# Two-row modulation runs, full-height blocks for the retention layer's 32 new tokens, full-row attention scores in the first half, and a new order table, in a one-core streaming-encoder step

## Chip, core and metric

The kernel runs on one core of one Trainium2 chip. Its metric is the device time of one execution in microseconds (us), lower being better. The core has five engines with instruction streams of their own: TensorE (PE in the profile; its weight loads are listed apart, as PEld), VectorE (DVE), ScalarE (ACT), GpSimd (POOL) and SyncE (SP, which here issues transfers). Each stream is static: an engine takes its instructions in the written order and waits at semaphores.

## The reference

One step of a two-layer streaming encoder on 512 prompt tokens and 32 new tokens, with 1024 features and fp32 throughout. Layer 0 mixes tokens by retention (8 heads, keys of 128, values of 256, a decayed state per head); after it one shared K and V is projected; layer 1 is differential attention (8 heads, each with two 64-wide halves) against that K and V. Each layer has a half-step SwiGLU FFN on either side of its mixer, a norm around each part, and shift, scale and gate from a conditioning vector.

```python
def modulate(x, g, shift, scale):
    return rms_norm(x, g) * (1 + scale[:, None, :]) + shift[:, None, :]

def swiglu(h, w_in, w_out):
    a, b = jnp.split(h @ w_in, 2, axis=-1)
    return (jax.nn.silu(a) * b) @ w_out

def retention_block(state, q, k, v, log_gamma):
    ...
    scores = jnp.einsum('bhid,bhjd->bhij', q, k) * d_intra
    out = (jnp.einsum('bhij,bhjv->bhiv', scores, v)
           + jnp.einsum('bhid,bhdv->bhiv', q * q_dec[..., None], state))
    new_state = state * c_dec[:, None, None] + jnp.einsum('bhjd,bhjv->bhdv', k * k_dec[..., None], v)
    return out, new_state
...
        logits = jnp.einsum('bqhtd,bkhtd->bhtqk', qblk, k).astype(jnp.float32) * (DH_B ** -0.5)
        p = jax.nn.softmax(jnp.where(visible, logits, -jnp.inf), axis=-1)
        pd = (p[:, :, 0] - lam * p[:, :, 1]).astype(v.dtype)
        return jnp.einsum('bhqk,bkhv->bqhv', pd, v)
```

The prompt passes through retention in chunks of 64 tokens, and the new tokens through one `retention_block` with the state that is given. The modulation is `silu(c) @ w_ada + b_ada`, nine vectors of 1024 for each layer and two for the shared K and V.

## The kernel before

**Layout.** Features lie on the 128 partitions and tokens on the columns. The tokens are in two halves: half 0 has 256 prompt tokens, half 1 the other 256 prompt tokens and the 32 new ones, 288 columns. Half 1 trails half 0 through the layers, so that one half's projections fill TensorE while the other waits for a norm.

**Main projections.** Weights come in tiles of 512 KB (eight contraction steps k, 128 features each; 384 KB for the last part of an FFN's down projection), issued by SP. ACT casts a tile to a high part (L576), DVE subtracts to get a low part (L579); four such pairs of slots, `WT`, exist. A *unit* is one 128-wide output feature block of one tile; with a half it is one run, `run_unit`: per k three matmuls (high weight by high and low operand, low weight by high operand, L597) into one PSUM bank. Five banks (ps_146 to ps_150 in the names) serve these runs, three (ps_151 to ps_153) everything else. A tile that both halves use closely after one another is cast once for both.

**Who sets the order.** A program at build time makes the order. `plan()` interleaves the units of both halves along a path, whose corner points come from the tables `BND` (layer 0, the shared K and V) and `ATT` (layer 1; `Q` is the query projection, `OB` the output projection of attention, `F2` the second FFN). Then a list scheduler with its own costs per instruction (`pe`, `act`, `dve`, `WAKE` and so on) lays every engine's stream down. `launch()` hands a unit a weight tile and a bank in planned order. The costs only shape the order; nothing of them runs.

**Around a projection.** `pre_ops` makes the operands of the next projection from the residual: the sum of squares over features goes to TensorE as a matmul with ones (L702), its power is taken by POOL (L708), the result is spread over the partitions by a transpose (L713), then per feature block a DVE multiply (L740), an ACT copy to the high part (L749) and a DVE subtraction (L755). Each output bank of a down projection is added up by DVE (L907 and L909) and squared and summed (L815, L819) on the way to the next such norm; `sub_end` applies that norm and adds to the residual (L868, L871). SwiGLU parts end in DVE and ACT steps that split the product again (L920, L921, L940 to L956).

**Modulation, L503.** For each of 9 pieces of 512 outputs per group, eight contraction steps, four matmuls each of 32 columns of the array (`PS[b][32*g:32*g+32]`, four column groups side by side). A step needs 1 MB of weights in one of two buffers (`NADA = 2`); a step was one entry of TensorE's order, so that most steps stood alone between main matmuls.

**Retention.** Per head: rotation of q and k (L1012 to L1026), transposes of v (`post_v`, L1071) and k (`ktok`, L1113), scores (L1202, L1203), outputs (L1219 to L1222), state (L1232), and `finish`, which norms and transposes back (L1172). The new tokens are a block of 32: their scores have 32 columns of the array (L1268), their outputs are a 32-column and a 32 by 32 matmul (L1277, L1278), their state update takes 32 rows (L1284), and their transposes are 32 wide.

**Attention scores.** Per head and block of 128 tokens, two matmuls of 64 rows each (L1535): q's halves stand on partitions 0 to 63 and 64 to 127, the two products go to two of the three misc banks. Mask (L1545), maximum (L1550), exponent (L1555), transposes (L1568), product with v (L1575), sub-norm (L1592, L1596), transpose to features (L1604) and the split for the output projection (L1610) follow. q is rotated with its rows permuted to match the K that is kept, which four transfers of 32 rows bring in (`ldk`).

Behind the change every line stands a few further down; those that matter are L503 (then L504), L597 (L599), L702 (L711), L713 (L722), L740 (L749), L755 (L764), L819 (L828), L868 and L871 (L877, L880), L909 (L918), L921 (L930), L941 (L950), L953 (L962), L579 (L581), L1604 (L1630).

## Time and profile before

| what | value |
|---|---|
| time, median of 3 runs | 2592.47 us (2589.95 to 2595.69) |
| time of the profiled execution | 2587.47 us |
| its span | 2585.5 us |
| mean TensorE clock granted in it | 0.995 |
| PE busy | 2515.2 us, 97% |
| DVE busy | 1415.6 us, 55% |
| ACT busy | 1088.6 us, 42% |
| moved by DMA | 408.41 MB, mean 158 GB/s |

The profiled execution is one run; its times are read against its own 2587.47 us, which is 1.98 us more than its span and 5.0 us less than the median. The engine rows give the time in which an engine was busy. TensorE's weight loads overlap its matmuls. The ends of matmuls are modelled, so that a matmul's own length overlaps the next one by a little; what a matmul costs is read from the starts of successive rows.

### The profile page before, as it was taken

To read this page: it belongs to the slowest core of one execution; us is meant where nothing else is said; L and a number is where in the kernel's file an instruction comes from. 1 tells how busy PE (TensorE), PEld (TensorE's weight loads), DVE (VectorE), ACT (ScalarE), POOL (GpSimd) and SP (SyncE) were. 2 spreads that over 40 slices of the span, in tenths; PEclk is the share of its full clock that TensorE was granted. 3 is DMA by queue.
4 is the path that set the end of the run, shared out by engine and by line. 5 is a ranking of instruction groups with operands and counts; after the bars stand their busy time and mean duration, and the time that the engine had idled before them with its cause. 6 is when DMAs were issued, how large, how long until landed. Compare 5 with 4: busy or idle time off the path is not lost.

```text
span 2585.5 us, 48240 instructions
## 1 busy us (share of the span) xinstructions
PE 2515.2 (97%) x19848; PEld 2366.4 (92%) x19848; DVE 1415.6 (55%) x2659; ACT 1088.6 (42%) x2150; POOL 57.6 (2%) x88
## 2 busy tenths in 40 slices
PE   6999999999999999999999999999999999999998
PEld 5899999789999997899998999999788988888998
DVE  5323336945424366323337945556875987658455
ACT  3222225643333364323126533444445655455434
POOL 0000000000000000000000000000000000000000
PEclk9999999999999999999999999999999999999999
DMA  8722224732222238622225754555754445545553
GB/s 338 265 90 86 87 99 137 263 128 95 78 86 81 74 134 333 245 83 90 99 78 196 256 182 134 171 177 182 277 198 147 152 158 179 176 151 168 166 169 108
DMA packets 123627, 408.41 MB, mean 158 GB/s; under 512 B 15504, under 2 KB 34064, under 8 KB 113168
## 3 DMA queue, kind: packets, MB, share of 16 engines
q1 hardware_dynamic: 123408, 405.35, 46.1%
q8 instruction: 155, 2.54, 0.4%
q14 instruction: 64, 0.52, 0.1%
HBM read 392.05 MB, written 13.24 MB: 157 GB/s over the span
## 4 chain that ended last, share of the span: by engine, by line
PE 64%; DVE 5%; DMA 2%; ACT 1%; issue 1%; POOL 0%; SPq 0%; POOLq 0%; DVEq 0%; ACTq 0%
PE ps L597 57%; DMA FA<-in_ada 1%; DVE w L579 1%; PE ps L503 1%; PE ps L1535 1%; ACT w L576 1%; PE ps L1575 1%; DVE r L755 1%; DVE FA L740 1%; DVE FA L1016 0%; PE ps L1702 0%; PE ps L1568 0%; DVE FA L819 0%; PE ps L1682 0%; PE ps L1642 0%
## 5 line engine op out<-in xcount | busy, mean ns | idle before, releaser
L597 PE MATMUL ps<-r,w 128*128 128x256 f32 (+1 forms) x17280 | 2274.9, 291 | 19.4 <-ACT r L920 4.9
L597 PEld LDWEIGHTS ps<-r,w 128*128 128x128 f32 x17280 | 2203.9, 191 | 92.8 <-issue 59.0
L579 DVE TENSOR_TENSOR w<-FA,w 128x1024 fp32r<-128x1024 f32 (+1 forms) x559 | 667.5, 1195 | 589.5 <-ACT w L576 586.9
L576 ACT CAST w<-FA 128x1024 fp32r<-128x1024 f32 (+1 forms) x559 | 572.2, 1024 | 949.6 <-PE ps L597 852.4
L956 DVE TENSOR_TENSOR FA<-ps,FA 128x256 f32<-128x256 f32 (+1 forms) x88 | 38.8, 441 | 172.4 <-PE ps L597 168.4
L920 ACT CAST r<-FA 128x256 fp32r<-128x256 f32 (+1 forms) x176 | 72.9, 416 | 107.3 <-DVE FA L956 85.9
L909 DVE TENSOR_TENSOR FA<-ps,FA 128x288 f32<-128x288 f32 (+1 forms) x144 | 62.7, 439 | 100.3 <-PE ps L597 98.8
L921 DVE TENSOR_TENSOR r<-FA,r 128x256 fp32r<-128x256 f32 (+1 forms) x176 | 76.5, 437 | 21.3 <-ACT r L920 21.2
L503 PE MATMUL ps<-FA,SC 128*32 128x512 f32 x576 | 77.0, 610 | 5.9 <-DMA FA<-in_ada 5.9
L749 ACT ACTIVATE r<-FA,MOD 128x256 fp32r<-128x256 f32 (+1 forms) x168 | 63.1, 436 | 43.7 <-DVE FA L740 43.5
L819 DVE TENSOR_TENSOR FA<-FA 128x256 f32<-128x256 f32 (+1 forms) x168 | 72.8, 435 | 13.0 <-ACT FA L815 11.5
L953 DVE SCALAR_TENSOR_TENSOR FA<-ps,FA 128x288 f32<-128x288 f32 (+1 forms) x88 | 38.3, 439 | 46.5 <-PE ps L597 46.3
L740 DVE SCALAR_TENSOR_TENSOR FA<-X,DRV,ps 128x256 f32<-128x256 f32 (+1 forms) x168 | 57.5, 396 | 8.8 <-PE ps L713 8.6
L849 ACT ACTIVATE FA<-FA,DRV 128x256 f32<-128x256 f32 (+1 forms) x144 | 59.1, 442 | 2.9
L755 DVE SCALAR_TENSOR_TENSOR r<-FA,MOD,r 128x256 fp32r<-128x256 f32 (+1 forms) x168 | 58.6, 400 | 3.1 <-ACT r L749 3.0
L944 ACT ACTIVATE FA<-ps 128x256 f32<-128x256 f32 (+1 forms) x88 | 34.5, 393 | 60.1 <-PE ps L597 60.0
L708 POOL TENSOR_TENSOR FA<-FA,NHALF 128x2 f32<-128x2 f32 (+1 forms) x24 | 19.9, 831 | 1748.1 <-DVE FA L706 926.2
L1016 DVE TENSOR_TENSOR FA<-ps,FA 64x288 f32<-64x288 f32 (+1 forms) x128 | 56.1, 438 | 2.1
L907 ACT COPY FA<-ps 128x288 f32<-128x288 f32 (+1 forms) x96 | 36.2, 380 | 43.2 <-PE ps L597 43.2
L1012 DVE TENSOR_TENSOR FA<-ps,FA 128x256 f32<-128x256 f32 (+1 forms) x64 | 28.0, 438 | 47.1 <-PE ps L597 46.7
L815 ACT ACTIVATE FA<-FA 128x256 f32<-128x256 f32 (+1 forms) x84 | 35.8, 426 | 14.9 <-DVE FA L909 14.4
L941 DVE SCALAR_TENSOR_TENSOR FA<-FA,ps 128x288 f32<-128x288 f32 (+1 forms) x88 | 37.7, 430 | 6.1 <-ACT FA L940 6.1
(145 smaller groups left out, 1083.0 us busy)
## 6 DMA issues: line engine op xcount, KB each, us to landing
FA<-in_w_ffn_in SPq DMA_DIRECT2D x266, 512.0 KB, 3.3
FA<-in_ada SPq DMA_DIRECT2D x80, 1024.0 KB, 7.1
FA<-in_w_ffn_out SPq DMA_DIRECT2D x96, 512.0 KB, 3.5
FA<-in_w_in_a SPq DMA_DIRECT2D x60, 512.0 KB, 3.2
FA<-in_w_ffn_out SPq DMA_DIRECT2D x61, 384.0 KB, 3.1
FA<-in_w_kv SPq DMA_DIRECT2D x23, 512.0 KB, 3.5
FA<-in_w_out_a SPq DMA_DIRECT2D x22, 512.0 KB, 3.4
FA<-in_w_q_b SPq DMA_DIRECT2D x16, 512.0 KB, 3.6
```

Source lines behind the costliest of these rows:

```text
L503: te.matmul(PS[b][32 * g:32 * g + 32, :], lhsT=SC[:, k, :], rhs=fa(ada_buf[u, k], 512, g * 512), start=(k == 0), stop=(k == 7))
L576: yield act(n, lambda: nc.scalar.copy(hi, src))
L579: yield dve(n, lambda: nc.vector.tensor_tensor(lo, src, hi.bitcast(F32), ALU.subtract))
L597: te.matmul(PS[b][:, :n], lhsT=w[:, a, k, :], rhs=x, start=(k == 0 and j == 0), stop=(k == u.nk - 1 and j == 2))
L740: nc.vector.scalar_tensor_tensor(fa(z, c1 - c0, o), X[:, f, c0:c1], DRV[:, gi, f, s:s + 1], PS[Rb][:, o:o + c1 - c0], ALU.mult, ALU.mult)
L749: nc.scalar.activation(op.hi(H, c0, c1), fa(z, c1 - c0, o), AF.Identity, bias=MOD[:, mi, f, s:s + 1])
L755: nc.vector.scalar_tensor_tensor(op.lo(H, c0, c1), fa(z, c1 - c0, o), MOD[:, mi, f, s:s + 1], op.hi(H, c0, c1).bitcast(F32), ALU.add, ALU. ...
L819: yield dve(n, lambda: nc.vector.tensor_tensor(acc, acc, fa(t), ALU.add))
L849: nc.scalar.activation(Y[:, f, c0:c1], Y[:, f, c0:c1], AF.Copy, scale=DRV[:, gg, f, s:s + 1])
L909: yield dvp(n, lambda: nc.vector.tensor_tensor(Y[:, f, c], PS[b][:, :n], Y[:, f, c], ALU.add), 15)
L920: yield act(n, lambda: nc.scalar.copy(op.hi(H), src), pr)
L921: yield dve(n, lambda: nc.vector.tensor_tensor(op.lo(H), src, op.hi(H).bitcast(F32), ALU.subtract), pr)
```

## The change

Four things change, and the order of everything is made anew.

**Modulation.** `ADA_K = 2`: one entry of TensorE's order now takes two contraction steps, and hands both buffers back behind the second. The same matmuls are done.

```diff
-            for k in range(8):
-                yield ada_ev[u, k]
-
-                def mm(u=u, k=k, b=b):
-                    for g in range(4):
-                        te.matmul(PS[b][32 * g:32 * g + 32, :], lhsT=SC[:, k, :],
-                                  rhs=fa(ada_buf[u, k], 512, g * 512), start=(k == 0), stop=(k == 7))
-                yield pe(980, mm, ADA_HI if u <= due[0] else ADA_LO)
-                ada_put(u, k)
+            for k0 in range(0, 8, ADA_K):
+                for k in range(k0, k0 + ADA_K):
+                    yield ada_ev[u, k]
+
+                def mm(u=u, k0=k0, b=b):
+                    for k in range(k0, k0 + ADA_K):
+                        for g in range(4):
+                            te.matmul(PS[b][32 * g:32 * g + 32, :], lhsT=SC[:, k, :],
+                                      rhs=fa(ada_buf[u, k], 512, g * 512), start=(k == 0), stop=(k == 7))
+                yield pe(TILED + ADA_K * 900, mm, ADA_HI if u <= due[0] else ADA_LO)
+                for k in range(k0, k0 + ADA_K):
+                    ada_put(u, k)
```

**Retention.** The 32 new tokens become the last 32 rows of a full block of 128 (the 96 prompt tokens ahead of them are computed along and not used; in the decay table and the masked scores they have zeros). All transposes and matmuls of that block are then 128 by 128, v and the scaled k are evacuated in one instruction rather than two, and DVE clears a 128 by 128 score block first.

```diff
+    LB = COLS[1].stop - COLS[1].start - P
+    SB = NTOK - P
+    def full_blocks(H):
+        return ((0, P), (P, P), (LB, P))[:2 + H]
...
-            yield pe(c_f(32, 32), lambda: te.matmul(PS[b][:NS_TOK, :NS_TOK], lhsT=V("k")[:, c0:c0 + NS_TOK],
-                                                           rhs=V("q")[:, c0:c0 + NS_TOK], start=True, stop=True), 500)
+            yield dve(P // 2, lambda: nc.vector.memset(sm, 0.0))
+            yield pe(c_f(P), lambda: te.matmul(PS[b][:, :NS_TOK], lhsT=V("k")[:, SB:], rhs=V("q")[:, c0:c0 + NS_TOK],
+                                               start=True, stop=True), 500)
...
-                te.matmul(o, lhsT=fa(qs, NS_TOK), rhs=V("st"), start=True, stop=False)
-                te.matmul(o, lhsT=fa(qs, NS_TOK, NS_TOK, 0, NS_TOK), rhs=vt()[:NS_TOK, 4, :], start=False, stop=True)
+                te.matmul(o, lhsT=qd, rhs=V("st"), start=True, stop=False)
+                te.matmul(o, lhsT=sm, rhs=vt()[:, 4, :], start=False, stop=True)
...
-            yield pe(c_f(256), lambda: te.matmul(PS[b2][:, :256], lhsT=kt()[:NS_TOK, 4, :], rhs=vt()[:NS_TOK, 4, :],
+            yield pe(c_f(256), lambda: te.matmul(PS[b2][:, :256], lhsT=kt()[:, 4, :], rhs=vt()[:, 4, :],
```

**Scores of half 0.** ACT makes two copies of q, each with the other half's rows at zero, and both products are matmuls of all 128 rows, into one bank; mask and maximum are one instruction each. Half 0's q and K need no permutation: 16 pairs of rotation steps on 32 rows fall away, and K comes by one transfer of 128 rows rather than four of 32. Half 1 is as before.

```diff
+            def cp():
+                for s in range(2):
+                    nc.scalar.activation(q3[:, s, :], qT, AF.Copy, scale=CT[:, C_MK + s:C_MK + s + 1])
+            yield ("ACT", 2 * c_act(P) + 180, cp)
+            bs = [(yield from anyb())]
+            l3 = PS[bs[0]][:, :2 * nk].rearrange("p (s n) -> p s n", s=2)
+            lg = [l3[:, 0], l3[:, 1]]
+            def qk():
+                for s in range(2):
+                    te.matmul(lg[s], lhsT=q3[:, s, :], rhs=kT[:, :nk], start=True, stop=True)
+            yield pe(2 * c_f(nk), qk, 500 + h)
```

**Tables and costs.** `TILED = 190` is added to the planner's cost of runs that use part of the array; `WAKE` 100 to 200, `ROPE_LEAD` 18 to 30, `CONV_P` -1 to 0, `ADA_LEAD` -40 to -52, `RETH` 3 to 4; `BND` and `ATT` have new numbers, of which one line:

```diff
-BND = {(0, 1): (7, 7, 7, 13), (0, 2): (6, 7, 8, 7), 'kv': (7, 8, 6, 7), (1, 0): (2, 2, 4, 6)}
+BND = {(0, 1): (7, 7, 6, 10), (0, 2): (7, 7, 6, 5), 'kv': (8, 8, 6, 8), (1, 0): (0, 1, 4, 6)}
```

In sum the modulation now stands in TensorE's order as 36 entries of 8 matmuls, where 66 of 4 and 3 of 8 stood; tiles cast fall from 559 to 552, and the DVE stream from 2661 instructions to 2606; ACT's goes from 2008 to 2017.

What the order looks like now at three places, which the prediction calls Q, end and OB:

*Q* is the start of layer 1's attention, where half 0's norm has to be finished before its query projection starts. TensorE there, before (ps_147 and ps_150 are half 1's down projection, ps_146 half 0's query projection, ps_153 the modulation, ps_152 the norm):

```order
L713 MATMUL ps_151<-CT,FA 128x128 x2
L597 MATMUL ps_147<-r_16_123,w_144 128x288
...
L503 MATMUL ps_153<-FA,SC 32x512 x8
L597 MATMUL ps_150<-r_2_109,w_144 128x288
...
L503 MATMUL ps_153<-FA,SC 32x512 x4
L702 MATMUL ps_152<-ONE,FA 32x2 x8
L713 MATMUL ps_152<-CT,FA 128x128 x2
L503 MATMUL ps_153<-FA,SC 32x512 x4
L597 MATMUL ps_146<-r_20_93,w_141 128x256
```

The same place after the change, nothing left out:

```order
L722 MATMUL ps_152<-CT,FA 128x128 x2
L599 MATMUL ps_150<-r_22_129,w_144 128x288
L599 MATMUL ps_150<-r_23_130,w_144 128x288
L599 MATMUL ps_150<-r_22_129,w_144 128x288
L599 MATMUL ps_150<-r_10_117,w_144 128x288
L599 MATMUL ps_150<-r_11_118,w_144 128x288
L599 MATMUL ps_150<-r_10_117,w_144 128x288
L504 MATMUL ps_151<-FA,SC 32x512 x8
L711 MATMUL ps_153<-ONE,FA 32x2 x8
L722 MATMUL ps_153<-CT,FA 128x128 x2
L599 MATMUL ps_146<-r_20_93,w_141 128x256
```

Between one norm's spreading transpose and the next norm's sums stood 39 main matmuls (15 and 24) and 12 of the modulation; now 6 and 8 stand there.

*End* is the last part of the last FFN, half 0, beside which DVE makes half 1's operands. DVE there, before (L909 with ps_148 and ps_150 empties banks for the next units; L953 and L921 make the last operands of half 0):

```order
L755 SCALAR_TENSOR_TENSOR r_7_114<-FA,MOD,r_6_113 128x256
L755 SCALAR_TENSOR_TENSOR r_7_114<-FA,MOD,r_6_113 128x32
L755 SCALAR_TENSOR_TENSOR r_17_124<-FA,MOD,r_16_123 128x256
L755 SCALAR_TENSOR_TENSOR r_17_124<-FA,MOD,r_16_123 128x32
L953 SCALAR_TENSOR_TENSOR FA<-ps_146,FA 128x256
L921 TENSOR_TENSOR r_11_84<-FA,r_10_83 128x256
L909 TENSOR_TENSOR FA<-ps_148,FA 128x256
L909 TENSOR_TENSOR FA<-ps_150,FA 128x256
```

And after; the 30 rows left out hold 25 further L749 and L764 steps (12 of 256 columns, 13 of 32) and five L581:

```order
L962 SCALAR_TENSOR_TENSOR FA<-ps_147,FA 128x256
L930 TENSOR_TENSOR r_23_96<-FA,r_22_95 128x256
L930 TENSOR_TENSOR r_11_84<-FA,r_10_83 128x256
L715 TENSOR_SCALAR FA<-ps_153 96x3
L918 TENSOR_TENSOR FA<-ps_150,FA 128x256
L581 TENSOR_TENSOR w_143<-FA,w_143 128x768
L749 SCALAR_TENSOR_TENSOR FA<-X,DRV,ps_153 128x256
...
L749 SCALAR_TENSOR_TENSOR FA<-X,DRV,ps_153 128x256
L749 SCALAR_TENSOR_TENSOR FA<-X,DRV,ps_153 128x32
L918 TENSOR_TENSOR FA<-ps_149,FA 128x256
```

The last operands have moved ahead of the block of L749 and L764, and one bank's emptying, that of ps_149, stays inside it.

*OB* is where half 0's attention output goes into its projection. TensorE before: the last head's transpose (L1604), and on the next row the main matmul that uses it:

```order
L597 MATMUL ps_148<-r_14_87,w_141 128x256
L1575 MATMUL ps_151<-FA 128x128 x2
L1604 MATMUL ps_153<-CT,FA 128x128 x2
L597 MATMUL ps_150<-r_30_103,w_142 128x256
L597 MATMUL ps_150<-r_31_104,w_142 128x256
```

After, the same transpose is followed by half 1's units (288 columns), and half 0's first output unit comes 184 rows later:

```order
L599 MATMUL ps_150<-r_14_121,w_143 128x288
L1630 MATMUL ps_153<-CT,FA 128x128 x2
L599 MATMUL ps_150<-r_30_137,w_143 128x288
...
L599 MATMUL ps_146<-r_2_109,w_144 128x288
...
L599 MATMUL ps_147<-r_8_81,w_141 128x256
```

The last head's whole chain now has other matmuls beside it, where its transpose and the matmul that uses it stood back to back.

More of the change, by code (lines that the diff above doesn't have):

```diff
@@ L34 @@
 C_KD = 192
-C_KDS = 208
 C_CO = 216
@@ L46 @@
 L0 = 1
-WAKE = 100
+WAKE = 200
 STREAM = 3
@@ L1141, in finish @@
         def finish(b, H, c0, n):
-            blks = ((0, P), (P, P)) if n == 256 else ((0, n),)
-            rows = blks[0][1]
-            nb = len(blks)
+            rows = P
+            nb = 2 if n == 256 else 1
+            w, o = (n, 0) if n == 256 else (P, P - n)
             og = yield from get(2 * n)
@@ L1171, in tr @@
                     for j in range(2):
-                        te.transpose(PS[b][:, j * n + i * P:j * n + i * P + rows],
-                                     fa(tk, P, 256 * i + j * P, 0, rows), CT[:rows, C_ID:C_ID + rows])
+                        te.transpose(PS[b][:, j * w + i * P:j * w + i * P + P], fa(tk, P, 256 * i + j * P), ID)
             yield pe(2 * nb * c_t(P), tr, 500)
@@ L1431, in post_q @@
                 yield at["qask"][H]
-                yield from rot(H, b, at["rope"], fa(at["q"][H], n, h * n), m=256)
+                yield from rot(H, b, at["rope"], fa(at["q"][H], n, h * n), m=256 * H)
                 S.set(at["hd"][h][H].q)
@@ L1524, in at_block @@
         yield ("get", at["bsem"], 1, 8 * H + h)
-        mem = yield from get(2 * nk + P + 16, h + H * .5)
+        mem = yield from get(2 * nk + P + 16 + (1 - H) * 256, h + H * .5)
         cut = lambda o, n: (mem[0] + o, n)
@@ L1529, in at_block, with qk @@
         p3 = fa(pp).rearrange("p (s n) -> p s n", s=2)
-        bs = yield ("get", miscb, 2, 0)
-        lg = [PS[b][:, :nk] for b in bs]
-        def qk():
-            for s in range(2):
-                te.matmul(lg[s], lhsT=qT[64 * s:64 * s + 64, :], rhs=kT[64 * s:64 * s + 64, :nk], start=True,
-                          stop=True)
-        yield pe(max(440, c_f(nk) + 10), qk, 500 + h)
+        if H:
+            bs = yield ("get", miscb, 2, 0)
+            lg = [PS[b][:, :nk] for b in bs]
+            def qk():
+                for s in range(2):
+                    te.matmul(lg[s], lhsT=qT[64 * s:64 * s + 64, :], rhs=kT[64 * s:64 * s + 64, :nk], start=True,
+                              stop=True)
+            yield pe(TILED + c_f(nk), qk, 500 + h)
+        else:
+            q3 = fa(cut(2 * nk + P + 16, 256)).rearrange("p (s m) -> p s m", m=P)
+            def cp():
[5 more added lines that the diff above has]
+            lg = [l3[:, 0], l3[:, 1]]
+            def qk():
+                for s in range(2):
+                    te.matmul(lg[s], lhsT=q3[:, s, :], rhs=kT[:, :nk], start=True, stop=True)
+            yield pe(2 * c_f(nk), qk, 500 + h)
         at["left"][H] -= 1
@@ L1543, in mask @@
         def mask():
-            for s in range(2):
-                nc.vector.memset(lg[s][0:64, nk - 64:], -3.0e38)
+            if H:
+                for s in range(2):
+                    nc.vector.memset(lg[s][0:64, nk - 64:], -3.0e38)
+            else:
+                nc.vector.memset(l3[0:64, :, nk - 64:], -3.0e38)
         yield ("DVE", 2 * c_dve(64), mask)
         def mx():
-            for s in range(2):
-                nc.vector.tensor_reduce(fa(m, 1, s), lg[s], AX.X, ALU.max, negate=True)
-        yield ("DVE", 2 * c_dve(nk), mx)
+            if H:
+                for s in range(2):
+                    nc.vector.tensor_reduce(fa(m, 1, s), lg[s], AX.X, ALU.max, negate=True)
+            else:
+                nc.vector.tensor_reduce(fa(m, 2), l3, AX.X, ALU.max, negate=True)
+        yield ("DVE", (1 + H) * 67 + 2 * nk / 0.96, mx)
         def ex():
@@ L1709, in at_sample @@
         b = yield from anyb()
-        yield pe(c_f(P), lambda: te.transpose(PS[b][:, :64], fa(t, P, P, 0, 64), CT[:64, C_ID:C_ID + 64]), 500)
+        yield pe(TILED + c_t(P), lambda: te.transpose(PS[b][:, :64], fa(t, P, P, 0, 64), CT[:64, C_ID:C_ID + 64]), 500)
         for j in range(2):
@@ L1799 @@
 DMA_LAT = 2500
-ROPE_LEAD = 18
+TILED = 190
+ADA_K = 2
+ROPE_LEAD = 30
 ADA_X = 4
@@ L1812 @@
 ADA_FIRST = 0
-ADA_LEAD = -40
+ADA_LEAD = -52
 ARENA_N = 20600
 YW = 2
-RETH = 3
+RETH = 4
 ATH = 3
```

77 lines of the change are left out of this document (37 added, 40 removed).

## Prediction

> **What bounds the kernel now.** I read the page's engine rows first, then TensorE's waits, the chain that ended last, and TensorE's timeline where the change acts. The page:
>
> ```profile
> PE 2515.2 (97%) x19848; PEld 2366.4 (92%) x19848; DVE 1415.6 (55%) x2659; ACT 1088.6 (42%) x2150; POOL 57.6 (2%) x88
> GB/s 338 265 90 86 87 99 137 263 128 95 78 86 81 74 134 333 245 83 90 99 78 196 256 182 134 171 177 182 277 198 147 152 158 179 176 151 168 166 169 108
> FA<-in_w_ffn_in SPq DMA_DIRECT2D x266, 512.0 KB, 3.3
> FA<-in_ada SPq DMA_DIRECT2D x80, 1024.0 KB, 7.1
> ```
>
> TensorE is busy for 97% of the span and no other engine for more than 55%, so the time is TensorE's work plus its waits. What it waits for (total us, times, longest):
>
> ```profile
> PE ps L702 <- DVE FA L819: 16.7, 7, 11.5
> PE ps L503 <- DMA FA<-in_ada: 5.9, 11, 1.4
> ```
>
> The waits are few and stand at stage borders. The price of a main matmul comes from a long undisturbed stretch: of 288 columns from the chain's last link (start, us, count), of 256 columns from TensorE's timeline (start, us, instruction, count).
>
> ```profile
> 2367.69 205.15 PE ps L597 x1551
> ```
>
> ```profile
> 2320.69 13.23 PE L597 MATMUL ps<-r,w 128*128 128x256 f32 x108
> 2333.85 0.36 PE L702 MATMUL ps<-ONE,FA 128*32 128x2 f32 x18
> ```
>
> 205.15/1551 is 0.132 us; (2333.85 - 2320.69)/108 is 0.122 us. The main matmuls are the same in number after the change. So three things can move the time: TensorE's other work, what it loses when it turns to that work and back, and the waits at borders. All prices below are distances between starts, since ends are modelled.
>
> **Modulation.** A step alone, then two in a row:
>
> ```profile
> 1018.51 2.25 PE L597 MATMUL ps<-r,w 128*128 128x288 f32 x15
> 1020.69 1.07 PE L503 MATMUL ps<-FA,SC 128*32 128x512 f32 x8
> 1021.68 5.30 PE L597 MATMUL ps<-r,w 128*128 128x288 f32 x39
> ...
> 968.32 1.92 PE L503 MATMUL ps<-FA,SC 128*32 128x512 f32 x16
> 970.17 4.93 PE L597 MATMUL ps<-r,w 128*128 128x256 f32 x39
> ```
>
> The 15 main matmuls ahead of the lone step should take 15 x 0.132 = 1.985 us and its start comes 2.18 us behind theirs: 0.195 us are lost in turning to a run that uses the array in column groups. The step is 0.99 us, so alone it costs 1.185. Two in a row are 1.85, with one turn 2.045. A pair saves 2 x 1.185 - 2.045 = 0.325 us. Of 66 lone steps 33 new pairs are made: 33 x 0.325 = 10.7 us. If the turn is lost anyway the saving is 2 x 0.99 - 1.85 = 0.13, in all 4.3. I take 10.7, since the lost 0.195 shows directly. The Trainium skill's page "TensorEngine Tiling (Array Packing)", Tiling Modes, Key Properties, says that a change of tiling mode drains TensorE; the 0.195 agrees, and by that rule 10.7 is the right end.
>
> The pair needs both its loads, and both buffers come free only behind it. Two loads are 2.1 MB; at the highest slice of the page, 338 GB/s, 6.2 us, and 512 KB with its 1.55 us at that rate lands after 3.3, so 1.75 are fixed: 8.0 us. In the new order most pairs stand 8.8 to 10.3 us of other TensorE work apart (counts by the prices above; the median is 9.2). So I cost the loads at nothing: that queued work hides them, with 1.2 us to spare.
>
> **Retention's new tokens.** Of one head, from the timeline:
>
> ```profile
> 810.16 0.59 PE L1220 MATMUL ps<-FA 128*128 128x256 f32 x2
> 810.59 0.59 PE L1222 MATMUL ps<-FA 128*128 128x256 f32 x2
> 811.11 0.62 PE L1277 MATMUL ps<-FA 128*32 128x256 f32 x2
> 811.66 0.61 PE L1278 MATMUL ps<-FA 32*32 32x256 f32 x2
> 812.21 2.42 PE L597 MATMUL ps<-r,w 128*128 128x256 f32 x18
> 814.47 1.02 PE L1232 MATMUL ps<-FA 128*128 128x256 f32 x4
> 815.42 0.69 PE L1284 MATMUL ps<-FA 32*128 32x256 f32 x2
> 816.05 0.63 PE L597 MATMUL ps<-r,w 128*128 128x256 f32 x3
> 816.51 0.84 PE L1172 MATMUL ps<-CT,FA 128*128 128x128 f32 x6
> ```
>
> A full fp32 matmul of 256 columns is 0.43 us (810.16 to 810.59; two records). From 810.59 to 814.47 are 3.88 us; less one such matmul and 18 x 0.122 = 2.20, L1277 and L1278 cost 1.25 with their turns. As full matmuls they cost 0.86: saved 0.39. From 814.47 to 816.51 are 2.04; less two full ones and 3 x 0.122, L1284 costs 0.81, and 0.43 as a full one: saved 0.38. The scores L1268 and the 32-row transposes in L1172 each stand for one turn of 0.195; I take 0.16 each, an estimate that leaves something for their added columns. A head saves 1.09, eight heads 8.7 us. Between nothing for those two (6.2) and the whole turn (9.3) lie the bounds. What DVE gains and loses here (a clear of 128 by 128 more, one evacuation less) lies beside TensorE's work on an engine at 55%.
>
> **Scores of half 0.** The pair of 64-row matmuls for 256 keys (one head's two halves, two records each):
>
> ```profile
> 1956.09 0.70 PE L1535 MATMUL ps<-FA 64*128 64x256 f32 x4
> 1956.72 1.06 PE L597 MATMUL ps<-r,w 128*128 128x288 f32 x6
> ```
>
> They take 0.63; two full ones in series take 0.86, 0.23 more, and one turn of 0.195 goes: 0.035 more in each of eight heads. For 128 keys half the surplus, 0.115, less the turn: 0.08 less in each of eight. The sum is -0.4 us, or +2.8 if no turn goes; I take 0. The Trainium skill's page "TensorE: Matmul & The Clock Gate", Part 3 on packing small matmuls, speaks against this part: matmuls in different row groups run together, in about the time of one. By it the pair would cost 0.43 and the change lose 0.43 and 0.215 per head, 5 us in all, and the forecast would be 2577; the trace's 0.63 lies between. The 32 copies on ACT (42% busy) and the shorter DVE stream lie off the path.
>
> **Borders.** At Q, half 0's norm, TensorE and then DVE:
>
> ```profile
> 1826.94 3.79 PE L597 MATMUL ps<-r,w 128*128 128x288 f32 x24
> 1831.00 1.07 PE L503 MATMUL ps<-FA,SC 128*32 128x512 f32 x8 [0.28 <-DMA FA<-in_ada]
> 1834.13 0.39 PE L702 MATMUL ps<-ONE,FA 128*32 128x2 f32 x16 [2.06 <-DVE FA L819]
> 1835.63 0.69 PE L713 MATMUL ps<-CT,FA 128*128 128x128 f32 x2 [1.11 <-POOL FA L708]
> 1836.25 1.94 PE L503 MATMUL ps<-FA,SC 128*32 128x512 f32 x8
> ```
>
> ```profile
> 1829.59 0.68 DVE L868 TENSOR_TENSOR FA<-FA,ps 128x512 f32<-128x512 f32 x1
> 1830.19 0.41 DVE L819 TENSOR_TENSOR FA<-FA 128x256 f32<-128x256 f32 x1
> 1830.53 0.68 DVE L871 TENSOR_TENSOR X<-X,FA 128x512 f32<-128x512 f32 x1
> ```
>
> TensorE waits 0.28 + 2.06 + 1.11 = 3.45 us. DVE has, from one norm to the next, four L868 and four L871 at 0.60, seven L819 at 0.34, one weight split and one small step (about 1.5): 8.7, and about 0.7 of handing over: 9.4. In the new order only 6 main matmuls and one pair of modulation steps stand beside that: 0.8 + 1.85 = 2.65. So TensorE waits about 6.7 for the sums, 1.1 for POOL, and, since nothing stands behind the spreading transpose where the 1.94 of L503 stood, about 1.9 for the operands: 9.7, that is 6.2 worse. After such a wait the clock drops, as the first of these rows shows (us; busy time of PE, PEld, DVE, ACT, POOL; PEclk; DMA share; GB/s), 0.52 over 7 us; I add 1 for that. The other two rows are OB and the second FFN of layer 1, F2:
>
> ```profile
> 1834.00:1841.00 7.00, 5.76 (x40) 3.68 (x41) 5.70 (x16) 3.04 (x7) 0.69 (x1) 0.52 0.87 312
> 1966.00:1981.00 15.00, 11.15 (x78) 9.90 (x79) 7.96 (x16) 9.68 (x24) 1.19 (x2) 1.00 0.41 137
> 2025.00:2037.00 12.00, 8.16 (x54) 7.75 (x52) 9.67 (x19) 9.09 (x22) 0.00 (x0) 0.86 0.40 138
> ```
>
> OB idles 3.85 us; with 184 rows of other matmuls behind the last transpose that goes: 3.8 gained. F2 idles 3.84 and loses up to 12 x 0.14 = 1.7 to the clock, since one bank's emptying stands behind a block of operand steps; in the new order 81 main matmuls (10.5 us) stand beside that block, and of the wait about 1 is left: 4.0 gained with 1.2 of the clock. At the end TensorE waits for the last operands of half 0, which stand behind operand steps of half 1; TensorE, then DVE:
>
> ```profile
> 2347.69 2.96 PE L597 MATMUL ps<-r,w 128*128 128x256 f32 x11 [4.92 <-ACT r L920]
> ```
>
> ```profile
> 2340.13 1.73 DVE L740 SCALAR_TENSOR_TENSOR FA<-X,DRV,ps 128x256 f32<-128x256 f32 x6
> 2346.78 0.42 DVE L953 SCALAR_TENSOR_TENSOR FA<-ps,FA 128x256 f32<-128x256 f32 x1
> ```
>
> Those operands now come ahead of the block, but bank ps_149 is emptied behind 28 of its steps, at (2346.78 - 2340.13)/24 = 0.28 each, and six weight splits of about 0.9: 13 us, beside which TensorE has 66 matmuls, 8 us. A wait of 5 takes the place of the 4.92: 0. Together the borders give -7.2 + 4.0 + 3.8 = 0.6 us.
>
> **The sum.** 10.7 + 8.7 + 0 + 0.6 = 20.0 us less: 2587.47 - 20.0 = 2567.5 for the profiled execution. That stands 5.0 below the median of the runs, 2592.47, so the forecast is 2572.
>
> **Rivals.** (1) *The pair's loads are late*, and the kernel slower. Both buffers come back together, so a pair's loads start only when the last pair ends; each weight tile ahead of them on SP's queue adds 1.55 us to the 8.0. With one ahead 9.5 stand against 8.8 to 10.3: about 0.5 late, 33 x 0.5 = 16, time 2588, no change. With two, 11.1: 1.9 late, 63 us, time 2635. It is slower from (2597.7 - 2572)/33 = 0.78 us late per pair on. For it: 7.1 us for a 1 MB load already. Against: 158 GB/s on average, and 11 waits of 69 now, 1.4 at most. One ahead 0.08, two 0.06. (2) *Turns cost nothing here*: modulation saves 4.3, L1268 and L1172 nothing, so 6.4 + 2.5 less: 2581. The 0.195 speaks against it: 0.12. (3) *Borders cost more*: the clock drops for two such stretches (7 us at 0.52, 3.4 each) behind Q's longer wait, where I count 1, and OB and F2 give half: 2572 + 5.8 + 3.9 = 2582; 0.10. (4) *Borders cost less*: Q's wait stays as it was and the end's goes: 2572 - 7.2 - 4.9 = 2560. For it: DVE may be ahead of its place in the order: 0.12. That the change isn't what it says is excluded by the order: 36 entries of modulation stand there.
>
> **The numbers.** The forecast has 0.52, with its own range 2563 to 2580 (retention 6.2 to 9.3, scores -0.4 to +2.8, borders 5 either way). A measurement can tell 0.2% of this kernel, 5.2 us, from no change: faster is below 2587.3, slower above 2597.7. Faster: 0.52 + 0.12 + 0.12, 0.07 of the 0.10 and 0.03 of the one-ahead case, 0.86. Same: the other 0.03 and 0.05, 0.08. Slower: 0.06. The range 2554 to 2588 leaves out the two-ahead case, half of the one-ahead case and the low end of (4).
>
> **What would show it.** Right: L504 rows of 16 records, each pair with the next main run about 2.05 us; no 32-row forms in retention, 0.43 us for each full one; a wait for L711 of 6 to 7 us at Q and one of about 5 for a bank at the end; none at OB. Wrong: waits of L504 for in_ada of over 10 us in all would show the first rival; a wait at Q of 3 or less the fourth; new waits at borders not named here, on other lines, would undo the sum.

## The result

The changed kernel takes 2562.45 us (median of 4 runs, 2562.03 to 2563.4), the kernel before 2591.92 (4 runs, 2589.95 to 2595.69): the ratio is 0.9885, 95% interval 0.9868 to 0.9902. The forecast was 2572, range 2554 to 2588: the sign and the range held, and the gain was 29.5 us where 20 were forecast.

The profiled execution of the changed kernel has a span of 2560.9 us, 24.6 less than the 2585.5 of before. The other 5 us lie in before's profiled execution, which at 2587.47 was faster than all four of its other runs. Its engine rows, then the three largest waits of TensorE (total us, times, longest):

```profile
PE 2496.2 (97%) x19848; PEld 2379.2 (93%) x19848; DVE 1400.1 (55%) x2604; ACT 1091.3 (43%) x2159; POOL 58.5 (2%) x88
```

```profile
PE ps L711 <- DVE FA L828: 15.0, 6, 11.2
PE ps L599 <- ACT r L758: 11.5, 5, 5.3
PE ps L504 <- DMA FA<-in_ada: 5.6, 3, 2.7
```

The 11.2 is the start of the program and stands in both kernels (11.5 before). L599's waits for L758 are 11.5 us in 5 places; before, the same wait (L597 for L749 there) was

```profile
PE ps L597 <- ACT r L749: 4.2, 2, 2.5
```

L504's wait is about as long as before (5.9 us there) but in 3 places instead of 11.

To see where the difference sits, I added up TensorE's records between its first and last main matmul. Each non-main record counts from its own start to the next one's, less any idle time of over 60 ns, which goes to the waits; a main matmul counts 0.132 or 0.120 us by its width (rounded here; 0.120 is the distance of two starts with nothing beside them), and what it takes beyond that, if it stands next to other work, goes to that work as its turn. What is left beyond is listed under "rest", with the first and small modulation steps, the transposes of modulation and tokens. In us:

| | before | changed | difference |
|---|---|---|---|
| main matmuls | 2179.3 | 2179.3 | 0 |
| modulation with its turns | 85.1 | 74.0 | -11.1 |
| retention with its turns | 99.9 | 92.0 | -7.9 |
| attention with its turns | 96.9 | 94.9 | -2.0 |
| norms with their turns | 17.1 | 20.0 | +2.9 |
| rest | 30.8 | 29.8 | -1.0 |
| waits | 42.7 | 36.8 | -5.9 |
| first to last main matmul | 2551.8 | 2526.8 | -25.0 |

The two large terms of the forecast, 10.7 for the modulation and 8.7 for retention, are there. A pair of modulation steps in the changed kernel, with main matmuls around it:

```profile
1002.27 7.22 PE L599 MATMUL ps<-r,w 128*128 128x288 f32 x54
1009.42 1.92 PE L504 MATMUL ps<-FA,SC 128*32 128x512 f32 x16
1011.28 0.98 PE L599 MATMUL ps<-r,w 128*128 128x256 f32 x6
```

The 16 records take 1.86 us from start to start, as the two adjoining steps of before did; over all 36 pairs a pair with its turns costs 74.0/36 = 2.06 us, and 2.045 were forecast. The same head's part of retention as the prediction shows of before:

```profile
809.30 0.59 PE L1221 MATMUL ps<-FA 128*128 128x256 f32 x2
809.73 0.59 PE L1279 MATMUL ps<-FA 128*128 128x256 f32 x2
810.16 0.59 PE L1280 MATMUL ps<-FA 128*128 128x256 f32 x2
810.40 2.50 PE L599 MATMUL ps<-r,w 128*128 128x256 f32 x18
812.82 1.13 PE L1231 MATMUL ps<-FA 128*128 128x256 f32 x4
813.78 0.59 PE L1286 MATMUL ps<-FA 128*128 128x256 f32 x2
814.03 0.70 PE L599 MATMUL ps<-r,w 128*128 128x256 f32 x3
814.57 0.83 PE L1172 MATMUL ps<-CT,FA 128*128 128x128 f32 x6
```

All forms are 128 by 128. From the first row to L1231 are 3.52 us where 3.88 stood, from there to the transposes 1.75 where 2.04 stood.

At Q the waits are shorter than forecast, 7.6 us and not 9.7, and their parts are other ones:

```profile
1800.31 1.93 PE L504 MATMUL ps<-FA,SC 128*32 128x512 f32 x16
...
1805.12 0.38 PE L722 MATMUL ps<-CT,FA 128*128 128x128 f32 x2
1805.26 1.04 PE L599 MATMUL ps<-r,w 128*128 128x288 f32 x6
1808.77 1.07 PE L504 MATMUL ps<-FA,SC 128*32 128x512 f32 x8 [2.47 <-DMA FA<-in_ada]
1812.51 1.94 PE L504 MATMUL ps<-FA,SC 128*32 128x512 f32 x8 [2.67 <-DMA FA<-in_ada]
1814.71 0.39 PE L711 MATMUL ps<-ONE,FA 128*32 128x2 f32 x16 [0.27 <-DVE FA L828]
1816.21 0.69 PE L722 MATMUL ps<-CT,FA 128*128 128x128 f32 x2 [1.11 <-POOL FA L717]
1818.02 7.73 PE L599 MATMUL ps<-r,w 128*128 128x256 f32 x39 [1.11 <-ACT r L758]
```

The modulation pair waits for its loads, 2.47 and 2.67 us, since the pair before it ended (1800.31 + 1.93) only 4.1 us before TensorE had nothing else to do (1805.26 + 1.04), and not the 8.8 to 10.3 us that the prediction counted for most pairs. But behind it the sums still wait 0.27 us for DVE. From the spreading transpose to the sums are 9.6 us, DVE's chain, for which 9.4 were forecast. All five waits make 7.6 us.

The granted clock behind it, and at the end (us, busy time of PE, PEld, DVE, ACT, POOL, PEclk, DMA share, GB/s):

```profile
1810.00:1824.00 14.00, 8.94 (x52) 6.43 (x53) 11.09 (x28) 5.28 (x14) 0.69 (x1) 0.51 0.53 207
2328.00:2336.00 8.00, 5.58 (x27) 5.62 (x28) 6.31 (x21) 4.14 (x10) 0.00 (x0) 0.57 0.21 72
```

TensorE is at half its clock for nearly 14 us at Q, twice as long as before.

The end, TensorE and then DVE:

```profile
2316.92 8.15 PE L599 MATMUL ps<-r,w 128*128 128x256 f32 x66
2330.42 11.30 PE L599 MATMUL ps<-r,w 128*128 128x256 f32 x69 [5.35 <-ACT r L758]
```

```profile
2328.76 1.18 DVE L749 SCALAR_TENSOR_TENSOR FA<-X,DRV,ps 128x256 f32<-128x256 f32 x4
2329.86 0.41 DVE L918 TENSOR_TENSOR FA<-ps,FA 128x256 f32<-128x256 f32 x1
```

Exactly the 66 main matmuls of the forecast pass, then TensorE idles 5.35 us. The profile names an ACT step as the releaser. But TensorE goes on at 2330.42, 0.15 us behind the end of the L918 that empties ps_149 (2329.86 + 0.41).

At OB and F2, from 1925 us to 2010 us, TensorE waits once:

```profile
1993.48 0.43 PE L722 MATMUL ps<-CT,FA 128*128 128x128 f32 x2 [0.94 <-POOL FA L717]
```

### The profile page after: what moved, and what is told of

Read it like the earlier page. It is cut to its first block, busy times and chain, and to the rows that moved or that the text cites. A ratio compares the mean times of both kernels' runs of the same rounds, so it can differ in the third digit from the quotient of the medians.

```text
span 2560.9 us, 48166 instructions
## 1 busy us (share of the span) xinstructions
PE 2496.2 (97%) x19848; PEld 2379.2 (93%) x19848; DVE 1400.1 (55%) x2604; ACT 1091.3 (43%) x2159; POOL 58.5 (2%) x88
## 4 chain that ended last, share of the span: by engine, by line
PE 86%; DVE 8%; ACT 3%; issue 2%; DMA 1%; POOL 0%; SPq 0%; POOLq 0%; DVEq 0%; ACTq 0%
PE ps L599 77%; DVE w L581 2%; PE ps L504 2%; ACT w L578 1%; DVE FA L1025 1%; DVE FA L749 1%; DVE r L764 1%; PE ps L1601 1%; PE ps L1231 1%; PE ps L1219 1%; ACT FA L858 0%; PE ps L1540 0%; DMA X<-in_xb 0%; PE ps L1594 0%; DVE FA L828 0%
## 5 line engine op out<-in xcount | busy, mean ns | idle before, releaser
L599 PE MATMUL ps<-r,w 128*128 128x256 f32 (+1 forms) x17280 | 2269.4, 291 | 15.8 <-ACT r L758 11.5
L599 PEld LDWEIGHTS ps<-r,w 128*128 128x128 f32 x17280 | 2205.5, 191 | 55.7 <-issue 25.9
L581 DVE TENSOR_TENSOR w<-FA,w 128x1024 fp32r<-128x1024 f32 (+1 forms) x552 | 658.9, 1194 | 572.4 <-ACT w L578 567.5
L578 ACT CAST w<-FA 128x1024 fp32r<-128x1024 f32 (+1 forms) x552 | 564.6, 1023 | 883.5 <-PE ps L599 799.8
L929 ACT CAST r<-FA 128x288 fp32r<-128x288 f32 (+1 forms) x176 | 73.1, 416 | 107.3 <-DVE FA L965 88.3
L918 DVE TENSOR_TENSOR FA<-ps,FA 128x288 f32<-128x288 f32 (+1 forms) x144 | 62.3, 438 | 97.7 <-PE ps L599 96.2
L930 DVE TENSOR_TENSOR r<-FA,r 128x288 fp32r<-128x288 f32 (+1 forms) x176 | 76.6, 437 | 21.9 <-ACT r L929 21.5
L758 ACT ACTIVATE r<-FA,MOD 128x256 fp32r<-128x256 f32 (+1 forms) x168 | 63.1, 437 | 51.7 <-DVE FA L749 51.3
L828 DVE TENSOR_TENSOR FA<-FA 128x256 f32<-128x256 f32 (+1 forms) x168 | 73.1, 436 | 12.7 <-ACT FA L824 11.1
L504 PE MATMUL ps<-FA,SC 128*32 128x512 f32 x576 | 70.7, 605 | 5.6 <-DMA FA<-in_ada 5.6
L953 ACT ACTIVATE FA<-ps 128x256 f32<-128x256 f32 (+1 forms) x88 | 34.5, 393 | 69.7 <-PE ps L599 69.6
L749 DVE SCALAR_TENSOR_TENSOR FA<-X,DRV,ps 128x256 f32<-128x256 f32 (+1 forms) x168 | 57.3, 396 | 9.5 <-PE ps L722 9.3
L764 DVE SCALAR_TENSOR_TENSOR r<-FA,MOD,r 128x256 fp32r<-128x256 f32 (+1 forms) x168 | 58.5, 400 | 0.4 <-ACT r L758 0.2
L504 PEld LDWEIGHTS ps<-FA,SC 128*32 128x32 f32 x576 | 14.8, 109 | 33.6 <-issue 22.4
```

The source lines that it names most:

```text
L504: te.matmul(PS[b][32 * g:32 * g + 32, :], lhsT=SC[:, k, :], rhs=fa(ada_buf[u, k], 512, g * 512), start=(k == 0), stop=(k == 7))
L578: yield act(n, lambda: nc.scalar.copy(hi, src))
L581: yield dve(n, lambda: nc.vector.tensor_tensor(lo, src, hi.bitcast(F32), ALU.subtract))
L599: te.matmul(PS[b][:, :n], lhsT=w[:, a, k, :], rhs=x, start=(k == 0 and j == 0), stop=(k == u.nk - 1 and j == 2))
L749: nc.vector.scalar_tensor_tensor(fa(z, c1 - c0, o), X[:, f, c0:c1], DRV[:, gi, f, s:s + 1], PS[Rb][:, o:o + c1 - c0], ALU.mult, ALU.mult)
L758: nc.scalar.activation(op.hi(H, c0, c1), fa(z, c1 - c0, o), AF.Identity, bias=MOD[:, mi, f, s:s + 1])
```

## The experiments

The theory after the result: modulation pairs and full-height retention blocks save what they save in turns, the scores of half 0 nothing, and the new order gains more than I had counted, though it is worse at Q. The rivals: turns cost nothing and it is all the new order; the borders' waits are not what I take them for. Every edit that touches the planner's input makes the order anew, so in each run the trace's sums are read beside the time.

**Single modulation steps.**

```diff
-ADA_K = 2
+ADA_K = 1
```

> The changed kernel with the modulation's runs put back to one contraction step each (69 entries instead of 36), everything else as changed; the order is planned anew. Theory: each lone step pays a turn of about 0.2 us into and out of its column groups, so 33 to 36 more turns and slower steps cost 10 to 12 us: 2573, and in the trace the modulation's rows with their turns sum to about 85 us instead of 74. Rival: turns cost nothing and the gain came from the new tables: 2562 to 2567, the sum about 78. Waits of these runs for their loads: at most as long as now (5.6 us), since each buffer comes back alone.

Measured: 2573.01 us (2571.39 to 2575.51), 10.6 above the changed kernel. Modulation with its turns sums to 86.5 us instead of 74.0. The waits for loads did not behave as expected, from TensorE's waits of this run:

```profile
PE ps L504 <- DMA FA<-in_ada: 16.0, 15, 2.7
```

They are 16.0 us in 15 places, not 5.6 in 3. The turns are real, since they stand in the rows. That the time rose by nearly as much is in part chance: against the 12.5 us in the rows stand 3.7 us more of waits in all and about 6 us less under "rest", half of it main matmuls in half-clock stretches (3.0 us beyond their price, where the changed kernel has 6.2). And pairs do not make the loads late here, they wait for them less often than single steps in the same tables.

**Retention's 32-row blocks back**, with all their old forms; everything else as changed.

```diff
-            yield pe(c_f(P), lambda: te.matmul(PS[b][:, :NS_TOK], lhsT=V("k")[:, SB:], rhs=V("q")[:, c0:c0 + NS_TOK],
+            yield pe(c_f(32, 32), lambda: te.matmul(PS[b][:NS_TOK, :NS_TOK], lhsT=V("k")[:, c0:c0 + NS_TOK],
...
-                te.matmul(o, lhsT=qd, rhs=V("st"), start=True, stop=False)
-                te.matmul(o, lhsT=sm, rhs=vt()[:, 4, :], start=False, stop=True)
+                te.matmul(o, lhsT=fa(qs, NS_TOK), rhs=V("st"), start=True, stop=False)
+                te.matmul(o, lhsT=fa(qs, NS_TOK, NS_TOK, 0, NS_TOK), rhs=vt()[:NS_TOK, 4, :], start=False, stop=True)
```

> The changed kernel with the retention layer's new tokens put back to blocks of 32 rows; the order is planned anew. Theory: 1.0 to 1.1 us of TensorE's time per head comes back, 8 heads: 2570 to 2571, with the outputs' two matmuls dearer by 0.4 us a head, the state's by 0.3 to 0.4, scores and transposes by 0.15 to 0.2 each. Rival: the retention stage is bound by its chain through DVE, and the partial matmuls only fill waits: 2562 to 2564.

Measured: 2570.32 us (2569.89 to 2571.11), 7.9 more. Retention with its turns is 100.1 us against 92.0, and the waits are the same within 0.7. The theory's number.

**Half 0's scores back to 64 rows**, the ACT copies and the K transfer with them.

```diff
-                for s in range(2):
-                    te.matmul(lg[s], lhsT=q3[:, s, :], rhs=kT[:, :nk], start=True, stop=True)
+                for s in range(2):
+                    te.matmul(lg[s], lhsT=qT[64 * s:64 * s + 64, :], rhs=kT[64 * s:64 * s + 64, :nk], start=True,
+                              stop=True)
```

> The changed kernel with half 0's attention scores put back to pairs of 64-row matmuls in two misc banks, q permuted and K in four transfers; the order is planned anew. Theory (the prediction's): no difference within 2 us, since the pair's 0.63 us with a turn stands against 0.86. Rival 1 (matmuls in different row groups run fully together): 5 us faster, 2557. Rival 2: the change's gain in attention, 2 us of TensorE rows and the shorter waits there, comes from this part: 2564 to 2568.

Measured: 2563.62 us (2562.68 to 2563.93), 1.2 more; attention with its turns 95.3 against 94.9. There is no gain of 5 us. Yet the two matmuls of a pair do run together in most of the pairs: in before's trace the four records of the pair that the prediction shows start at 0, 0.007, 0.320 and 0.327 us, and the next matmul at 0.63. One 64-row matmul alone takes 0.63 us too (the run with the 64-row state update, below: 815.71 to 816.34). What uses the gain up is that a 64-row matmul between full ones takes 0.63 where a full one takes 0.43. Of the 2.0 us that attention lost between the two kernels 0.4 come from this part.

**Banks emptied first**, in the last part of every down and output projection.

```diff
-                    yield dvp(n, lambda: nc.vector.tensor_tensor(Y[:, f, c], PS[b][:, :n], Y[:, f, c], ALU.add), 15)
+                    yield dvp(n, lambda: nc.vector.tensor_tensor(Y[:, f, c], PS[b][:, :n], Y[:, f, c], ALU.add), -2 if last else 15)
```

> The changed kernel with one number of the planner changed: DVE's emptying of a bank in the last part of a down projection (L918) goes ahead of operand steps rather than behind them. Theory: the wait of 5.35 us in the last FFN is for bank ps_149, whose emptying stands behind 28 operand steps, and TensorE runs at half clock for 6.8 us behind it; both go, together 5.4 + 3.4: 2553 to 2555. Rival: the wait is for the operands (the profile names ACT's L758 as the releaser), which come no earlier: 2561 to 2563.

Measured: 2565.52 us (2564.2 to 2566.67), 3.1 slower. The same stretch of TensorE in this run:

```profile
2318.41 14.59 PE L599 MATMUL ps<-r,w 128*128 128x256 f32 x118
2333.76 6.96 PE L599 MATMUL ps<-r,w 128*128 128x288 f32 x47 [0.76 <-DVE r L764]
...
2353.45 8.82 PE L599 MATMUL ps<-r,w 128*128 128x288 f32 x49 [4.47 <-DVE FA L950]
```

118 main matmuls now run without the gap that stood behind the 66th, so the wait was for the bank, against the rival and against the releaser that the profile named. But the time did not come: 4.47 us came back 20 us later, where half 1's next bank is emptied by an L950 that stands behind half 0's last residual steps on DVE. And the number acts in other stages as well: at the border near 466 us, in layer 0, the waits grew from 1.4 to 4.7 us, with 6.8 us of half clock that the changed kernel does not have there, which is the size of the loss. The cause of the wait at the end is shown; that this edit would pay was wrong.

**A hold at Q.** One corner of the path more, five of half 1's units wide:

```diff
-ATT = [(Q, -67, Q, -75), (Q, 4, Q, -34), (Q, 8, Q, -23), (OB, 0, Q, -31), (OB, -8, Q, -13), (F2, 1, Q, -16),
+ATT = [(Q, -67, Q, -75), (Q, 0, Q, -40), (Q, 0, Q, -35), (Q, 4, Q, -34), (Q, 8, Q, -23), (OB, 0, Q, -31), (OB, -8, Q, -13), (F2, 1, Q, -16),
```

> The changed kernel with one corner of the path at Q altered: half 0 holds for five of half 1's units between its last output unit and its first query unit, so that about 93 of half 1's matmuls (12 us) stand between the norm's spreading transpose and the next sums rather than 6 and a modulation pair. Theory: DVE's chain of 9.4 us is then covered, the waits at Q (2.47 + 2.67 + 0.27 + 1.11 + 1.11 = 7.6 us) shrink to at most 1, and the half-clock stretch of 13.7 us behind them (6.8 lost) goes: 12 to 14 us faster, 2549 to 2551. Rival 1: the five units are missing in the attention stage, whose waits grow by as much: 2558 to 2563. Rival 2: the waits go, the half-clock stretch stays where it is: 2555 to 2557.

Measured: 2552.04 us (2550.74 to 2555.43), 10.4 below the changed kernel and not the 12 to 14 of the theory. TensorE at the same border, and the window in which the changed kernel was at half clock:

```profile
1802.53 0.31 PE L711 MATMUL ps<-ONE,FA 128*32 128x2 f32 x16 [0.99 <-DVE FA L828]
1802.76 1.86 PE L599 MATMUL ps<-r,w 128*128 128x288 f32 x12
1805.37 0.43 PE L722 MATMUL ps<-CT,FA 128*128 128x128 f32 x2 [0.75 <-POOL FA L717]
```

```profile
1810.00:1824.00 14.00, 14.00 (x111) 12.05 (x110) 13.16 (x28) 6.73 (x13) 0.00 (x0) 1.00 0.78 288
```

Of 7.6 us of waits 1.7 are left, and the clock stays at 1.00. So Q cost the changed kernel some 10 us, waits and clock together. The hold covers DVE's chain and also moves the modulation pairs apart (this run has no wait of L504 over 0.15 us), so it does not tell the one from the other. Nothing of size was missed in attention: with its turns 95.8 against 94.9. The hold does not change the number of main matmuls or of casts (552).

**The same with three units:**

```diff
-ATT = [(Q, -67, Q, -75), (Q, 4, Q, -34), (Q, 8, Q, -23), (OB, 0, Q, -31), (OB, -8, Q, -13), (F2, 1, Q, -16),
+ATT = [(Q, -67, Q, -75), (Q, 0, Q, -39), (Q, 0, Q, -36), (Q, 4, Q, -34), (Q, 8, Q, -23), (OB, 0, Q, -31), (OB, -8, Q, -13), (F2, 1, Q, -16),
```

> The same with a hold of three units of half 1 rather than five, 10.4 us of TensorE's work beside DVE's 9.4. Theory: as the hold of five, the cover being just enough: within 2 us of it. Rival: if the units are missed in attention, this one loses fewer and is 2 to 5 us faster than the hold of five; if the cover is too short, it keeps 1 to 3 us of wait and part of the half clock, and is 3 to 6 us slower.

Measured: 2553.13 us (2551.32 to 2554.1): within 1.1 us of the five, and the two ranges overlap. Ten us of cover are enough for a chain of 9.4.

**The tables alone.** The kernel before, with the numbers of `BND`, `ATT`, `WAKE`, `ROPE_LEAD`, `CONV_P`, `ADA_LEAD`, `RETH` and the added costs, and nothing else.

```diff
-WAKE = 100
+WAKE = 200
...
-ROPE_LEAD = 18
+TILED = 190
+ROPE_LEAD = 30
```

> The kernel before with the new tables and planner costs alone: no pairs, retention's 32-row blocks, half 0's old scores. Theory from the three single reversals (10.6, 7.9 and 1.2 us): the parts add up, and the tables are worth the remaining 9 to 11 us: 2582 to 2584. The prediction's step said 0.6 us slower for the borders: 2592 to 2594. Rival: the tables only suit the new parts, and alone make it slower than before: over 2597.

Measured: 2579.57 us (2579.37 to 2581.02) against 2591.6 for before beside it: ratio 0.9954, interval 0.9939 to 0.9969. The tables are worth 12.0 us by themselves, more than the 9 to 11 of the theory. (The prediction's borders were a gain of 0.6 us, not the loss that the expectation speaks of.) About 4 of the 12 go with the clock: the four runs have a mean granted clock of 0.994 to 0.995, before's runs beside them 0.991 to 0.994, and the two profiled executions, both at 0.995, are 8.1 us apart (2579.37 and 2587.47). In the trace its attention is 3.4 us cheaper than before's (93.5 against 96.9), the rest 6.8 (24.0 against 30.8), the waits 1.0; norms, modulation and retention are about 2 dearer. Of the 6.8, 3.1 are main matmuls in half-clock stretches (5.7 us beyond their price before, 2.6 here). With the three reversals (10.6, 7.9, 1.2) the parts add up to 31.7, where 29.5 were measured together.

**One matmul's form, the order kept.** The state update takes 64 of its 128 rows; the rows left out are zeros in the scaled k.

```diff
-            yield pe(c_f(256), lambda: te.matmul(PS[b2][:, :256], lhsT=kt()[:, 4, :], rhs=vt()[:, 4, :],
+            yield pe(c_f(256), lambda: te.matmul(PS[b2][:, :256], lhsT=kt()[64:, 4, :], rhs=vt()[64:, 4, :],
```

> The changed kernel with one matmul's form changed and every engine's order kept: the state update of the new tokens (L1286) takes the last 64 rows of its block rather than all 128 (the 64 left out hold zeros of the scaled k, so nothing is lost). Theory: the form alone costs a turn, 0.2 to 0.4 us each time, 8 heads: 1.5 to 3 us in the trace's rows of L1231 and L1286, the time 2564 to 2565. Rival: half the rows cost no more than all, and turns come from something else (the new order): no difference in these rows, 2562.5.

Measured: 2565.3 us (2563.39 to 2566.55), 2.9 more. The rows of this run:

```profile
814.65 1.13 PE L1231 MATMUL ps<-FA 128*128 128x256 f32 x4
815.71 0.70 PE L1286 MATMUL ps<-FA 64*128 64x256 f32 x2
816.34 0.62 PE L599 MATMUL ps<-r,w 128*128 128x256 f32 x3
```

From L1231 to the main matmuls are 1.69 us where the full form needs 1.21 (812.82 to 814.03); retention with its turns is 95.0 us against 92.0, 3.0/8 = 0.37 a time. Half the rows cost more than all. About 0.20 of the 0.37 lies in the matmul itself (815.71 to 816.34 are 0.63, a full one is 0.43), the rest in its neighbours. Here nothing but the form changed: every engine's instructions stand in the same order in both traces. So this is the cleanest measure of a turn, and the rival is out.

**Three attempts to go on from the hold.** Every step of layer 1's second FFN that empties a bank first, for both halves:

```diff
+        pr = -2 if l == 1 and j == 1 else 20
...
-                        yield act(n, lambda: nc.scalar.activation(fa(t), PS[b][:, :n], AF.Tanh, scale=0.5))
+                        yield act(n, lambda: nc.scalar.activation(fa(t), PS[b][:, :n], AF.Tanh, scale=0.5), pr)
```

> The hold of five at Q, and in layer 1's second FFN every step that empties a bank (L918, and the tanh, L950 and L962 steps on a bank, one line lower here) goes ahead of other DVE and ACT work, for both halves. Emptying L918 alone first removed the wait of 5.35 us at the end, and 4.5 us came back at an L950 behind half 0's last residual steps. Theory: the banks alone are what TensorE waits for at the end; with L950 first too, neither wait is left, nor the half-clock stretch of 6.8 us: 5 + 3.4 us off the 2552 of the hold alone: 2543 to 2545. Rival: DVE has more work there than TensorE can cover, and the wait comes back for operands or weights: 2550 to 2553.

Measured: 2551.04 us (2548.97 to 2553.02), 1.0 below the hold alone, the ranges overlapping. TensorE at the end:

```profile
2314.05 17.76 PE L599 MATMUL ps<-r,w 128*128 128x256 f32 x139
...
2338.47 21.69 PE L599 MATMUL ps<-r,w 128*128 128x288 f32 x162 [1.48 <-DVE w L581]
```

139 main matmuls without a gap, and no 4.5 us at L950. What is left are waits of 0.2 to 1.5 us for weights and operands. The waits for banks went as in the theory, and the time is the rival's: all of TensorE's waits, counted as in the table, are 29.2 us where the hold alone has 30.7. In its profiled execution, the slowest of the four, half-clock stretches stand at three other places instead, 13.7 us in all as with the hold alone.

The same in both FFNs of layer 1:

```diff
-        pr = -2 if l == 1 and j == 1 else 20
+        pr = -2 if l == 1 else 20
```

> The same in both FFNs of layer 1. Theory: Q's and F2's borders have their waits covered already with the hold, so no more than 1 us from the kernel with the second FFN alone. Rival: the steps put back (residual and norm) come later and a border's wait grows by 2 to 4 us.

Measured: 2551.58 us (2550.09 to 2554.41): no difference from the former. The rival's wait did come, at Q, where the waits grew from 0.6 to 2.9 us, and one of 2.0 us near 2009 went.

Two more units of half 0 beside half 1's norm at the second border of layer 0:

```diff
-BND = {(0, 1): (7, 7, 6, 10), (0, 2): (7, 7, 6, 5), 'kv': (8, 8, 6, 8), (1, 0): (0, 1, 4, 6)}
+BND = {(0, 1): (7, 7, 6, 10), (0, 2): (7, 7, 8, 5), 'kv': (8, 8, 6, 8), (1, 0): (0, 1, 4, 6)}
```

> The hold of five at Q, and in the second border of layer 0 (retention to the second FFN) half 0 runs eight units rather than six beside half 1's norm. There TensorE waits 1.7 us for ACT's L758 and 1.1 for L764, and the clock is halved for 3.4 to 6.8 us behind it. Theory: two more units (5.9 us) cover it: the waits of 2.8 and 2 to 3 for the clock go, 2547 to 2549. Rival: the wait is not one of cover (bank or slot), or comes back on the other half: 2551 to 2553.

Measured: 2549.0 us (2547.8 to 2549.99), 3.0 below the hold alone. That border in this run, with no wait in it:

```profile
993.20 0.41 PE L722 MATMUL ps<-CT,FA 96*128 96x96 f32 x3
993.40 5.90 PE L599 MATMUL ps<-r,w 128*128 128x256 f32 x42
```

All three together:

> The three edits together: the hold of five at Q, two more units of cover at the second border of layer 0, banks emptied first in layer 1's second FFN. Theory: they act on different borders and add up: the hold with the cover was 2549.0, and the end's wait of 5.4 and half-clock stretch go but for some 2 us: 2543 to 2546. Rival: the half-clock stretches come back at other short waits, as they did with the banks emptied first, and nothing is left of it: 2548 to 2551.

Measured: 2547.28 us (5 runs, 2546.45 to 2550.19), ratio to before 0.9831, interval 0.9817 to 0.9846. It is the fastest kernel of the study, 15.2 us below the changed one. Against the hold with the cover it gains 1.7, with overlapping ranges, not the 3 to 6 of the theory. Its mean granted clock is 0.998, and the stretch at Q is at full clock (as all of it, up to the tail):

```profile
1810.00:1824.00 14.00, 14.00 (x106) 11.90 (x104) 12.40 (x27) 9.62 (x24) 0.00 (x0) 1.00 0.75 256
```

So the rival, half-clock stretches coming back, is not what held it: there are none. Waits came back instead. Counted as in the table they are 25.8 us, and 26.3 in the run with the hold and the cover: the 5.4 at the end are gone, and in their place stand several of 0.4 to 0.6 us and this one, for a weight split:

```profile
2332.73 2.55 PE L599 MATMUL ps<-r,w 128*128 128x288 f32 x17 [1.49 <-DVE w L581]
```

## Why the prediction was right, and where its size was off

- *Modulation, 10.7.* Right in mechanism and size: 11.1 in the rows. Undone, it is 12.5 in the rows and 10.6 in time, the latter with waits and clock mixed in. The lower bound, 4.3, is out.
- *The pair's loads at nothing, and rival 1.* Right: 5.6 us of waits for them in all, 5.1 of these at Q beside a chain that takes as long anyway. That pair stands closer to the one before it than I had counted. I also had not seen that single steps in the new tables would wait 16 us: there pairing helps the loads, though both buffers come back together.
- *Retention, 8.7.* Right, a little high: 7.9 in the rows and 7.9 in time. The outputs gave 0.36 a head (0.39 forecast) and the state 0.29 (0.38): I had put to the state's turn the 0.09 by which L1232's four records ahead of it (0.95) exceed two full matmuls (0.86); they still exceed them in the changed kernel (0.96).
- *Scores, 0.* Right: undone, the rows cost 0.4 us more, the lower of my bounds for the part (-0.4 to +2.8), and the time is 1.2 us more with overlapping ranges. By the packing rule of the Trainium skill's page "TensorE: Matmul & The Clock Gate", Part 3, matmuls in different row groups run together, in about the time of one. The trace agrees: the pair takes 0.63 us and one 64-row matmul alone 0.63. But I had put the price of a full matmul, 0.43, for that one, and the 5 us of this rival came from there; the run gained nothing.
- *Borders named.* Q was forecast 7.2 us worse: waits 7.6 against 3.45, 4.2 more, and 6.8 us more of half clock, 3.4 lost: 7.6 in all. The waits were shorter than forecast (7.6, not 9.7) and the clock cost more than the 1 us I gave it, which belong together: the second step of the pair took 1.94 us at half clock where the first took 1.07, and so covered more of the chain. The hold took 10.4 us out again, about what Q costs. OB's waits are gone, as forecast. F2 has 0.9 left, as forecast. At the end 4.92 was replaced by 5.35 from the place that was named. One sign of being wrong did appear, a new wait at a border that was not named: near 994 us, in layer 0, 1.66 and 0.53 us with 3.4 us of half clock. It did not undo the sum; covering it gained 3.0 us on top of the hold.
- *The step that failed is the term "borders, 0.6 us gained" as the whole worth of the new order.* The tables alone gained 12.0 us, 8.1 between profiled executions of one mean clock. The four borders that I costed came out much as forecast; I left the rest of the order at nothing, and it holds the difference. In the tables-alone trace it lies in attention's rows and turns (3.4) and in the rest (6.8), of which 3.1 are main matmuls that no longer run at half clock and the others small pieces all over. Which of the numbers does it is open: the table set was only tried as a whole.
- *The profiled run and the median.* I added 5.0 us for the difference of before's profiled execution from its median, as a constant. In the changed kernel the profiled execution was a median one (2562.68). Of the 9.5 us that the forecast was high, 5 are this, and the other 4.5 are what the order saved beyond my sum.
- *Rival 4 (borders cost less)* came nearest in its number, 2560, by the wrong way, which is luck: Q's wait did not stay, and the end's did not go.
